# The first tile's early store, the late weights and the zeroes of a two-expert combine

## The chip, the cores and the metric

The kernel runs on one core of one Trainium2 chip. The metric is device time in microseconds (us) of the slowest core, which here is the only one. The kernel before took 238.82 us, the median of 3 runs (238.82 to 239.0).

## The reference

Each of 16 x 1024 = 16384 tokens has the output rows of two experts (k = 2), 512 float32 values each, and two weights. The result is the weighted sum of the two rows.

```python
# expert_outputs (16, 1024, 2, 512), combine_weights (16, 1024, 2), float32
weights = combine_weights[..., np.newaxis]
return np.sum(expert_outputs * weights, axis=2).astype(np.float32)
```

The inputs are 67.1 MB and the output is 33.6 MB, so 100.8 MB cross between HBM and SBUF, with two multiplications and one addition for each output value.

## The kernel before, in words

**Layout.** The 128 partitions hold 128 tokens each. A partition's tokens t = 0 to 114 ("main") are neighbours in HBM; the last 13 tokens of each partition come from a second block behind the first. A tile is 13 (or 12) tokens of every partition: 10 tiles, g = 0 to 9, of 13, 13, 12, 13, 13, 13, 12, 13, 13 and 13 tokens. One big SBUF tensor, `et`, has four rooms of 13, 13, 12 and 13 tokens; tile g lives in room g mod 4. So tiles 0 to 3 are loaded at the start, and tile g + 4 can only be loaded when the store of tile g has read its results out of the room. The results stand in the room itself: the sums are written, packed, to its first half. `halves` is the same tensor seen as rows of 512 values, two to a token.

**Engines and queues.** SP issues all the loads (line 76), in five pieces at first (2, 11, 13, 12, 13 tokens: the first tile is cut in two), then one for each tile from 4 to 9, each behind the store that frees its room. SP's DMAs are queue q1 of the profile. ACT (ScalarE) issues, on queue q10, a small store of zeroes to 16 places of the output that are overwritten later (line 111), the weights of tiles 0 to 8 (line 79, called on line 112), the weights of tile 9 in two halves of 64 partitions (line 114), a warm-up activation (line 115), and the stores of tiles 0 to 6 (line 130). The stores of tiles 7 and 8 together, and of tile 9, go out on SP instead. The zeroes are set by DVE (VectorE) on line 108.

**Arithmetic.** Tiles 0 to 7 ("WHOLE") take two DVE instructions each: a product of all the tile's values with the weights, in place (line 88), and a sum of the two halves of each token (line 97). Tile 8 ("MIXED") has part of its products on ACT (line 92) and the rest on DVE (lines 94 and 96). Tile 9 goes token by token: ACT scales one half (line 102), DVE multiplies the other and adds (line 103).

**Order.** The program order is written out by hand (`manual_schedule`): the zeroes, the weights, the five first loads, and then for each store in the list `STORES` its tile's arithmetic, the store, and the load into the room that it frees. Each engine runs its own part of that list in order; semaphores hold an instruction until what it needs has landed or has been read.

Of the kernel before, what the change touches and what calls it, by code (L numbers as in the profile page):

```python
# [1 line left out]

# [4 lines left out]


@with_exitstack
def kernel(  # L10
    ctx: ExitStack,
    tc: tile.TileContext,
    expert_outputs: bass.AP,
    combine_weights: bass.AP,
    out: bass.AP,
):

    nc = tc.nc
    b, s, k, h = expert_outputs.shape
    assert k == 2
    n = b * s
    P = nc.NUM_PARTITIONS
    per = n // P
    assert per * P == n

    ROOM = [13, 13, 12, 13]
    ROOMS = len(ROOM)  # L30
    SITE = [sum(ROOM[:i]) for i in range(ROOMS)]
    TILES = [13, 13, 12, 13, 13, 13, 12, 13, 13, 13]
    FIRST = [2, 11, 13, 12, 13]
    STORES = [[0], [1], [2], [3], [4], [5], [6], [7, 8], [9]]
    WHOLE = [0, 1, 2, 3, 4, 5, 6, 7]
    MIXED = [8]
    ALONE = 3
    FREE = {9: 0}
    LAST = 13
    assert all(c <= ROOM[g % ROOMS] for g, c in enumerate(TILES))  # L40
    assert sum(TILES) == per and [g for st in STORES for g in st] == list(range(len(TILES)))
    main = per - LAST
    starts = [sum(TILES[:g]) for g in range(len(TILES))]

    def rows(x):

        first = x[0 : P * main, :].rearrange("(p t) f -> p t f", p=P)
        second = x[P * main : n, :].rearrange("(p t) f -> p t f", p=P)
        return lambda t, c: first[:, t : t + c, :] if t < main else second[:, t - main : t - main + c, :]

    flat = out.rearrange("b s h -> (b s) h")
    eo = rows(expert_outputs.rearrange("b s k h -> (b s) (k h)"))
    cw = rows(combine_weights.rearrange("b s k -> (b s) k"))
    o = rows(flat)

    dt = mybir.dt.float32
    mult = mybir.AluOpType.mult
    add = mybir.AluOpType.add
    copy = mybir.ActivationFunctionType.Copy

    pool = ctx.enter_context(tc.tile_pool(name="all", bufs=1))
    et = pool.tile([P, sum(ROOM), k * h], dt)
    halves = et.rearrange("p j (k h) -> p (j k) h", k=k)
    wt = pool.tile([P, per * k], dt)
    wk = wt.rearrange("p (t k) -> p t k", k=k)
    zt = pool.tile([16, 128], dt)
    warm = pool.tile([P, 1], dt)

    def place(t):
        g = max(g for g in range(len(TILES)) if starts[g] <= t)  # L70
        return SITE[g % ROOMS] + t - starts[g]

    def load(t, c, **kw):
        at = place(t)
        assert place(t + c - 1) == at + c - 1
        nc.sync.dma_start(out=et[:, at : at + c], in_=eo(t, c), **kw)  # L76

    def weights(q, t, c):
        q.dma_start(out=wk[:, t : t + c, :], in_=cw(t, c))

    def combine(g, base):
        at, c, t0 = SITE[g % ROOMS], TILES[g], starts[g]
        if g in WHOLE or g in MIXED:
            room = halves[:, k * at : k * (at + c), :]
            x0, x1 = et[:, at : at + c, 0:h], et[:, at : at + c, h : 2 * h]
            if g in WHOLE:
                wb = wt[:, k * t0 : k * (t0 + c)].unsqueeze(2).to_broadcast([P, k * c, h])
                nc.vector.tensor_tensor(out=room, in0=room, in1=wb, op=mult)  # L88
            else:
                for i in range(ALONE, c):  # L90
                    x = et[:, at + i, 0:h]
                    nc.scalar.activation(out=x, in_=x, func=copy, scale=wt[:, k * (t0 + i) : k * (t0 + i) + 1])  # L92
                w1 = wk[:, t0 : t0 + c, 1:2].to_broadcast([P, c, h])
                nc.vector.tensor_tensor(out=x1, in0=x1, in1=w1, op=mult)  # L94
                w0 = wk[:, t0 : t0 + ALONE, 0:1].to_broadcast([P, ALONE, h])
                nc.vector.tensor_tensor(out=x0[:, 0:ALONE], in0=x0[:, 0:ALONE], in1=w0, op=mult)  # L96
            nc.vector.tensor_tensor(out=halves[:, base : base + c, :], in0=x0, in1=x1, op=add)  # L97
            return
        for i in range(c):
            t = k * (t0 + i)  # L100
            x0, x1 = halves[:, k * (at + i), :], halves[:, k * (at + i) + 1, :]
            nc.scalar.activation(out=x0, in_=x0, func=copy, scale=wt[:, t : t + 1])  # L102
            nc.vector.scalar_tensor_tensor(  # L103
                out=halves[:, base + i, :], in0=x1, scalar=wt[:, t + 1 : t + 2], in1=x0, op0=mult, op1=add
            )

    with tc.manual_schedule():
        nc.vector.memset(zt, 0.0)  # L108

        ahead = flat[0 : P * main, :].rearrange("(q t) h -> q (t h)", q=16)  # L110
        nc.scalar.dma_start(out=ahead[:, 0:128], in_=zt)  # L111
        weights(nc.scalar, 0, main)
        for half in (slice(0, P // 2), slice(P // 2, P)):
            nc.scalar.dma_start(out=wk[half, main:per, :], in_=cw(main, per - main)[half])
        nc.scalar.activation(out=warm, in_=nc.const_aps.tensor(1.0, (P, 1), dt), func=copy)  # L115

        t = 0
        for i, c in enumerate(FIRST):
            load(t, c, **({"max_dma_last_dim": k * h * 4} if i == 0 else {}))
            t += c  # L120
        assert t == sum(TILES[:ROOMS])
        for j, st in enumerate(STORES):
            room = FREE.get(st[0], st[0] % ROOMS)
            base, c = SITE[room] * k, 0
            for g in st:
                combine(g, base + c)
                c += TILES[g]
            assert c <= k * ROOM[room]
            q = nc.sync if j in (7, 8) else nc.scalar
            q.dma_start(out=o(starts[st[0]], c), in_=halves[:, base : base + c, :])  # L130
            for g in st:
                if g + ROOMS < len(TILES):
                    load(starts[g + ROOMS], TILES[g + ROOMS])


# [1 line left out]
_INS = ['expert_outputs', 'combine_weights']  # L137
_OUTS = [((16, 1024, 512), 'float32')]


# [23 lines left out]
```

## Time and profile before

| what | value |
|---|---|
| time, median of 3 runs | 238.82 us (238.82 to 239.0) |
| profiled execution: span from first to last instruction | 237.1 us |
| HBM read, written | 67.24 MB, 33.56 MB |
| DVE busy in the span | 190.0 us |
| ACT busy in the span | 15.8 us |

Of the profiled execution the span is all that is recorded; its own time as a run is not listed. The 1.7 us between its span and the median of the runs lie before the first instruction and after the last one.

How to read it: times are microseconds from the start of the span unless marked ns. A row of the timeline or the groups names the engine, the line of the kernel, the operation, what is written from what, and the shapes. ACTq and SPq are the instructions by which ACT and SP issue DMAs. "To landing" is the time from a DMA's issue until its last byte and its semaphore have arrived. The windows view gives, for a stretch of the span, the busy time of each engine, the mean busy share of the 16 DMA engines, and the GB/s that they moved. It counts a packet where it starts, so that short stretches come out lumpy: a packet here can be one partition's whole row of a tile.

### The profile page before, as it was taken

How to read it: one execution, taken by the hardware profiler on the slowest of the kernel's cores; microseconds unless marked ns; L12 is line 12 of the kernel's file. 1: busy time of each engine (PE TensorE's matmuls, PEld its weight loads, DVE VectorE, ACT ScalarE, POOL GpSimd, SP SyncE). 2: the span in 40 equal slices, each digit the busy share in tenths (PEclk: the TensorE clock that was granted, in tenths of full speed). 3: DMA queues.
4: the chain of work that ended last, by engine and by line, in shares of the span. 5: the costliest groups of instructions: out<-in, count | busy, mean ns of one | idle time of the engine just before them, and what ended most of it. 6: DMA issues, size and time to landing. Idle time of an engine off the chain costs nothing.

```text
span 237.1 us, 154 instructions
## 1 busy us (share of the span) xinstructions
DVE 190.0 (80%) x33; ACT 15.8 (7%) x25; POOL 0.2 (0%) x4
## 2 busy tenths in 40 slices
DVE  0006999999999999999999998998499969919400
ACT  2000000000000000000000000000000055019200
POOL 0000000000000000000000000000000000000000
DMA  8999999989999999999899999999899999899996
GB/s 300 388 481 434 432 421 398 470 348 485 449 431 458 431 440 390 486 420 420 359 492 409 409 509 392 431 503 431 359 431 503 420 397 483 381 431 431 431 431 287
DMA packets 3344, 100.80 MB, mean 425 GB/s; under 512 B 512, under 2 KB 656, under 8 KB 912
## 3 DMA queue, kind: packets, MB, share of 16 engines
q1 hardware_dynamic: 2000, 77.33, 75.9%
q10 hardware_dynamic: 1344, 23.47, 23.0%
HBM read 67.24 MB, written 33.56 MB: 425 GB/s over the span
## 4 chain that ended last, share of the span: by engine, by line
DVE 55%; DMA 36%; issue 1%; ACT 0%; DVEq 0%; ACTq 0%; SPq 0%
DVE et L88 35%; DVE et L97 17%; DMA out_dram<-et 17%; DMA et<-in_expert_outputs_dram 12%; DMA wt<-in_combine_weights_dram 8%; DVE et L103 3%; ACT et L102 0%; DVEq L159 0%; ACTq L111 0%; DVE zt L108 0%; DVEq L88 0%; SPq L76 0%; ACTq L102 0%
## 5 line engine op out<-in xcount | busy, mean ns | idle before, releaser
L88 DVE TENSOR_TENSOR et<-et,wt 128x13312 f32<-128x13312 f32 (+1 forms) x8 | 110.0, 13754 | 23.8 <-DMA wt<-in_combine_weights_dram 18.7
L97 DVE TENSOR_TENSOR et<-et 128x6656 f32<-128x6656 f32 (+1 forms) x9 | 62.8, 6973 | 0.4
L92 ACT ACTIVATE et<-et,wt 128x512 f32<-128x512 f32 x10 | 6.2, 708 | 188.0 <-DMA et<-in_expert_outputs_dram 188.0
L103 DVE SCALAR_TENSOR_TENSOR et<-et,wt 128x512 f32<-128x512 f32 x13 | 8.7, 747 | 5.0 <-ACT et L102 5.0
L102 ACT ACTIVATE et<-et,wt 128x512 f32<-128x512 f32 x13 | 8.1, 707 | 14.0 <-DMA et<-in_expert_outputs_dram 14.0
L94 DVE TENSOR_TENSOR et<-et,wt 128x6656 f32<-128x6656 f32 x1 | 7.1, 7093 | 2.3 <-DMA et<-in_expert_outputs_dram 2.3
L96 DVE TENSOR_TENSOR et<-et,wt 128x1536 f32<-128x1536 f32 x1 | 1.8, 1751 | 0.0
L115 ACT ACT_TABLE_LOAD x1 | 1.3, 1283 | 3.1 <-issue 3.1
L108 DVE MEMSET zt<- 16x128 f32 x1 | 0.2, 165 | 0.8 <-PEq L148 0.8
L115 ACT ACTIVATE warm<-const-float32-1.0 128x1 f32<-128x1 f32 x1 | 0.2, 203 | 0.0
L148 POOL MEMSET const-bfloat16-1.0<- 128x1 bf16 x1 | 0.1, 102 | 0.0
L148 POOL MEMSET const-uint8-127<- 128x1 uint8 x1 | 0.1, 101 | 0.0
L148 POOL MEMSET const-float32-0.0<- 128x1 f32 x1 | 0.1, 99 | 0.2 <-issue 0.2
L148 POOL MEMSET const-float32-1.0<- 128x1 f32 x1 | 0.1, 98 | 0.0
## 6 DMA issues: line engine op xcount, KB each, us to landing
et<-in_expert_outputs_dram SPq DMA_DIRECT2D x7, 6656.0 KB, 32.2
out_dram<-et ACTq DMA_DIRECT2D x5, 3328.0 KB, 34.7
et<-in_expert_outputs_dram SPq DMA_DIRECT2D x2, 6144.0 KB, 41.1
out_dram<-et SPq DMA_DIRECT2D x1, 6656.0 KB, 19.9
out_dram<-et ACTq DMA_DIRECT2D x2, 3072.0 KB, 37.2
et<-in_expert_outputs_dram SPq DMA_DIRECT2D x1, 5632.0 KB, 18.2
out_dram<-et SPq DMA_DIRECT2D x1, 3328.0 KB, 14.0
et<-in_expert_outputs_dram SPq DMA_DIRECT2D x1, 1024.0 KB, 5.0
```

The costliest lines, as they stand in the source:

```text
L88: nc.vector.tensor_tensor(out=room, in0=room, in1=wb, op=mult)
L92: nc.scalar.activation(out=x, in_=x, func=copy, scale=wt[:, k * (t0 + i) : k * (t0 + i) + 1])
L94: nc.vector.tensor_tensor(out=x1, in0=x1, in1=w1, op=mult)
L96: nc.vector.tensor_tensor(out=x0[:, 0:ALONE], in0=x0[:, 0:ALONE], in1=w0, op=mult)
L97: nc.vector.tensor_tensor(out=halves[:, base : base + c, :], in0=x0, in1=x1, op=add)
L102: nc.scalar.activation(out=x0, in_=x0, func=copy, scale=wt[:, t : t + 1])
L103: nc.vector.scalar_tensor_tensor(out=halves[:, base + i, :], in0=x1, scalar=wt[:, t + 1 : t + 2], in1=x0, op0=mult, op1=add)
L108: nc.vector.memset(zt, 0.0)
L115: nc.scalar.activation(out=warm, in_=nc.const_aps.tensor(1.0, (P, 1), dt), func=copy)
L148: nc = _bacc.Bacc("TRN2", target_bir_lowering=False, num_devices=1)
```

## The change

Three edits, all in the first tile and the set-up.

1. The first tile's first 3 tokens (`EARLY`) get a product and a sum of their own and are stored by ACT at once. The product, the sum and the store for the other 10 tokens follow. The store's two parts go to the same places of the output as the one store did.
2. The weights of the last tile are loaded by one DMA of 128 partitions, issued by ACT right behind the second part of the first tile's store, in place of two DMAs of 64 partitions at the start.
3. The zeroes are set by GpSimd (POOL in the profile) in place of DVE.

The rest of the diff moves the same instructions into helpers (`products`, `sums`, `store`); for tiles 1 to 9 they are the same instructions in the same order.

```diff
+    EARLY = 3
...
+    def products(room, t, c):
+        wb = wt[:, k * t : k * (t + c)].unsqueeze(2).to_broadcast([P, k * c, h])
+        nc.vector.tensor_tensor(out=room, in0=room, in1=wb, op=mult)
+
+    def sums(at, c, base):
+        x0, x1 = et[:, at : at + c, 0:h], et[:, at : at + c, h : 2 * h]
+        nc.vector.tensor_tensor(out=halves[:, base : base + c, :], in0=x0, in1=x1, op=add)
+
-    def combine(g, base):
-        at, c, t0 = SITE[g % ROOMS], TILES[g], starts[g]
+    def combine(g, base, done=0):
+        at, c, t0 = SITE[g % ROOMS] + done, TILES[g] - done, starts[g] + done
+        if g in WHOLE:
+            products(halves[:, k * at : k * (at + c), :], t0, c)
+            sums(at, c, base)
+            return
...
+    def store(q, t, base, c):
+        q.dma_start(out=o(t, c), in_=halves[:, base : base + c, :])
+
     with tc.manual_schedule():
-        nc.vector.memset(zt, 0.0)
-
+        nc.gpsimd.memset(zt, 0.0)
         ahead = flat[0 : P * main, :].rearrange("(q t) h -> q (t h)", q=16)
         nc.scalar.dma_start(out=ahead[:, 0:128], in_=zt)
         weights(nc.scalar, 0, main)
-        for half in (slice(0, P // 2), slice(P // 2, P)):
-            nc.scalar.dma_start(out=wk[half, main:per, :], in_=cw(main, per - main)[half])
         nc.scalar.activation(out=warm, in_=nc.const_aps.tensor(1.0, (P, 1), dt), func=copy)
...
+        early = EARLY
+        products(halves[:, k * SITE[0] : k * (SITE[0] + early), :], 0, early)
+        sums(SITE[0], early, k * SITE[0])
+        store(nc.scalar, 0, k * SITE[0], early)
         for j, st in enumerate(STORES):
             room = FREE.get(st[0], st[0] % ROOMS)
             base, c = SITE[room] * k, 0
+            done = early if j == 0 else 0
             for g in st:
-                combine(g, base + c)
+                combine(g, base + c + done, done)
                 c += TILES[g]
...
-            q = nc.sync if j in (7, 8) else nc.scalar
-            q.dma_start(out=o(starts[st[0]], c), in_=halves[:, base : base + c, :])
+            store(nc.sync if j in (7, 8) else nc.scalar, starts[st[0]] + done, base + done, c - done)
+            if j == 0:
+                weights(nc.scalar, main, per - main)
```

More of the change, by code (lines that the diff above doesn't have):

```diff
@@ L79, in weights @@
         q.dma_start(out=wk[:, t : t + c, :], in_=cw(t, c))
-    def combine(g, base):
-        at, c, t0 = SITE[g % ROOMS], TILES[g], starts[g]
-        if g in WHOLE or g in MIXED:
-            room = halves[:, k * at : k * (at + c), :]
-            x0, x1 = et[:, at : at + c, 0:h], et[:, at : at + c, h : 2 * h]
[L86 to L97, printed above, removed]
+    def products(room, t, c):
+        wb = wt[:, k * t : k * (t + c)].unsqueeze(2).to_broadcast([P, k * c, h])
+        nc.vector.tensor_tensor(out=room, in0=room, in1=wb, op=mult)
```

9 lines of the change are left out of this document (added).

## The prediction, on record before the result

> **What bounds the kernel now.** I read the page first: its span, its slices and its queues.
>
> ```profile
> span 237.1 us, 154 instructions
> DVE 190.0 (80%) x33; ACT 15.8 (7%) x25; POOL 0.2 (0%) x4
> DMA  8999999989999999999899999999899999899996
> DMA packets 3344, 100.80 MB, mean 425 GB/s; under 512 B 512, under 2 KB 656, under 8 KB 912
> q1 hardware_dynamic: 2000, 77.33, 75.9%
> q10 hardware_dynamic: 1344, 23.47, 23.0%
> ```
>
> DVE is busy for 80% of the span, but the DMA engines for 75.9 + 23.0 = 98.9%. The windows view cuts off the ends and tells where the missing 1.1% lies (columns: window, length, DVE, ACT and POOL busy, clock, DMA share, GB/s).
>
> ```profile
> 2.00:235.70 233.70, 189.85 (x32) 15.79 (x25) 0.00 (x0) 1.00 1.00 431
> 235.70:237.10 1.40, 0.00 (x0) 0.00 (x0) 0.00 (x0) 1.00 0.00 0
> 213.00:222.00 9.00, 8.44 (x13) 7.88 (x13) 0.00 (x0) 1.00 1.01 438
> 43.40:45.70 2.30, 2.30 (x1) 0.00 (x0) 0.00 (x0) 1.00 0.96 342
> ```
>
> From 2.0 to 235.7 us the DMA share is 1.00 at 431 GB/s. So the span is 2.0 us of start, 233.7 us of transfers without a hole, and 1.4 us of end. The chain of waits names DVE for much of the span; I don't follow it, because a saved microsecond of DVE leaves the same bytes to be moved. The time can fall only if the bytes move faster or the ends shrink, and can rise only if the engines stand idle or get more work.
>
> The second thing to see is how the two queues share the engines. These are rows of the DMA view (KB each, us to landing), and q1 and q10 in the window 20.5 to 36 us (packets, MB, share).
>
> ```profile
> et<-in_expert_outputs_dram SPq DMA_DIRECT2D x1, 5632.0 KB, 18.2
> wt<-in_combine_weights_dram ACTq DMA_DIRECT2D x1, 115.0 KB, 18.2
> wt<-in_combine_weights_dram ACTq DMA_DIRECT2D x2, 6.5 KB, 31.0
> out_dram<-zt ACTq DMA_DIRECT2D x1, 8.0 KB, 3.9
> et<-in_expert_outputs_dram SPq DMA_DIRECT2D x7, 6656.0 KB, 32.2
> out_dram<-et SPq DMA_DIRECT2D x1, 6656.0 KB, 19.9
> ...
> q1 hardware_dynamic: 144, 6.75, 100.6%
> q10 hardware_dynamic: 144, 0.01, 0.7%
> ```
>
> 115 KB of weights land as late as 5632 KB of data, and in 15.5 us both queues start 144 packets, though one moves 6.75 MB and the other 0.01. The engines take turns, a packet from each queue, whatever its size: a tiny row waits for one big row of the other queue. 144 packets are 9 for each of 16 engines, for 128 rows 8 and one completion. At 431 GB/s, 26.9 for an engine, a row of a 13-token load (53,248 B) takes 1.98 us, of its store half of that, 0.99 us, of a 12-token load 1.83 us and store 0.91 us.
>
> **The change, part by part.** The rows for DVE and for the issues (start, us, what; idle time in brackets):
>
> ```profile
> 0.33 0.10 POOL L148 MEMSET const-uint8-127<- 128x1 uint8 x1
> 0.81 0.17 DVE L108 MEMSET zt<- 16x128 f32 x1 [0.81 <-PEq L148]
> 1.91 1.16 ACTq L114 DMA_DIRECT2D wt<-in_combine_weights_dram  x2
> 19.73 14.02 DVE L88 TENSOR_TENSOR et<-et,wt 128x13312 f32<-128x13312 f32 x1 [18.75 <-DMA wt<-in_combine_weights_dram]
> 33.78 7.09 DVE L97 TENSOR_TENSOR et<-et 128x6656 f32<-128x6656 f32 x1
> 40.91 0.34 ACTq L130 DMA_DIRECT2D out_dram<-et  x1
> 61.86 12.95 DVE L88 TENSOR_TENSOR et<-et,wt 128x12288 f32<-128x12288 f32 x1
> 74.84 6.56 DVE L97 TENSOR_TENSOR et<-et 128x6144 f32<-128x6144 f32 x1
> 145.69 12.96 DVE L88 TENSOR_TENSOR et<-et,wt 128x12288 f32<-128x12288 f32 x1 [1.10 <-DMA et<-in_expert_outputs_dram]
> 169.18 14.03 DVE L88 TENSOR_TENSOR et<-et,wt 128x13312 f32<-128x13312 f32 x1 [3.94 <-DMA et<-in_expert_outputs_dram]
> 192.63 7.09 DVE L94 TENSOR_TENSOR et<-et,wt 128x6656 f32<-128x6656 f32 x1 [2.30 <-DMA et<-in_expert_outputs_dram]
> 199.64 1.75 DVE L96 TENSOR_TENSOR et<-et,wt 128x1536 f32<-128x1536 f32 x1
> ```
>
> *DVE.* 14.02 against 12.95 us is 1.04 ns a value and 0.1 to 0.2 us fixed. Products of 3 and 10 tokens then take 3.4 and 10.8 us; sums 1.75 (the 1536-value row) and 5.5 us (7.09 against 6.56 gives the same slope). Together 21.4 against 21.1 us: +0.3 us for every later tile. The wait of 1.10 us before tile 6, then 3.94 and 2.30 us, hide it; without them it would cost 0.3 us.
>
> *The early store.* Its arithmetic starts at 19.73 as before (token 2 comes with the 11-token load), so ACT issues it at 24.9, and the other 10 tokens' at 41.2. Neither adds bytes. It adds 128 rows, 8 for an engine. What a row costs beyond its bytes the trace doesn't list. From below it is nothing. From above: at the best stretch's 438 GB/s, 100.8 MB take 230.1 us of the 233.7; put the whole rest, 3.6 us, on 3344 / 16 = 209 packets, and it is 0.017 us each, 0.14 us for 8. I take 0.1. The number of DMAs stays the same (one store more, one weight load less). A small gain can't be excluded: at 43.4 to 45.7, where the first store's rows begin, the rate is 342, worth (431 - 342) / 431 x 2.3 = 0.5 us. The early store may only move that hitch; I count it at 0 and keep 0.5.
>
> *The last weights.* Two issues of together 1.16 us leave ACT's start, where only the warm-up stands behind them. Their 128 rows need as many turns as before, 9, but now in q10 behind the first tile's store and ahead of tile 1's. That has to be followed:
>
> ```profile
> q10 hardware_dynamic: 15, 0.40, 92.5%
> ...
> 61.97 0.34 ACTq L130 DMA_DIRECT2D out_dram<-et  x1
> 67.80 0.33 SPq L76 DMA_DIRECT2D et<-in_expert_outputs_dram  x1
> 81.43 0.34 ACTq L130 DMA_DIRECT2D out_dram<-et  x1
> 91.42 0.33 SPq L76 DMA_DIRECT2D et<-in_expert_outputs_dram  x1
> 123.44 14.02 DVE L88 TENSOR_TENSOR et<-et,wt 128x13312 f32<-128x13312 f32 x1
> 208.61 14.02 SPq L130 DMA_DIRECT2D out_dram<-et  x2
> 183.92 28.80 DMA et<-in_expert_outputs_dram
> 212.72 0.02 issue
> ```
>
> The first row is q10 between 45 and 46 us: the store issued at 40.91 starts its rows there, 4.8 us after its issue. So the early store starts near 30 and, with 8 turns of 1.9 + 0.23 us, is through by about 47. The second part follows, 8 turns of 1.9 + 0.76 us: about 68, where the whole store landed before (SP's refill of room 0 goes out at 67.80). Then the weights hold q10 for their 8 rows with 7 load rows of 1.98 us between, 14 us, to 82. Tile 1's store, issued near 62.3, had its turns from 68 on; now it starts 14 us later. In those 14 us the loads have the engines nearly alone. Four of tile 4's rows are in by 82 and the other four, in turns with tile 1's store (2.97 us each), by 94, instead of 67.8 + 32.2 = 100. Then SP has nothing to load until tile 1's store is in: its last 4 rows run unshared, to 98 (before: 91.4). The load of tile 5 goes out at 98 and starts between 99 (1 us later, an estimate) and 103 (4.8 us, as above); tile 2's store, issued at 81.8, holds 8 x 0.91 = 7.3 us of rows, to 105. So the engines have work throughout. With 8 turns of 1.98 + 0.95 us tile 5 is in between 122.5 and 126.5, against 123.8 on DVE (123.44 + 0.3): at worst 2.7 us late, which the same three waits (7.3 us) hide. From there the old rhythm runs on.
>
> *The zeroes.* POOL's rows show 0.10 us for a memset of 128x1, DVE's 0.17 us for this one; on POOL it may take 0.1 to 1.3 us (the longest small instruction here, ACT's table load, is under 1.3 us). If the weights lose a turn by it, DVE starts 1.7 us later (an 11-token row); the waits of 1.10 + 3.94 + 2.30 = 7.3 us hide that. Loads don't wait for the zeroes. Counted at 0.
>
> *The end.* The last load lands at 212.72. The stores of tiles 7 and 8 have been issued at 208.61, 4.1 us ahead, and tile 9's goes out 14.0 us later, at 222.3, while the pair's 6656 KB land 19.9 us after their issue, at 228.5. So DVE could be late by 7.3 + 4.1 = 11.4 us at tile 1 before the engines ran dry here.
>
> Sum: 0 (DVE) + 0.1 (rows) + 0 (weights) + 0 (zeroes) = +0.1 us on the span of 237.1, and with the same 1.7 us outside it, 238.9 us.
>
> **The rivals.**
>
> *Faster: the hitch of the first store goes.* For it: the 342 GB/s row. Against: a first store remains, and packets of 2 us make so short a window lumpy. Worth 0.5 us, or up to 0.7 if the end also gets shorter: 238.3, 238.1 at best.
>
> *Slower: the parked weights starve the rooms.* Place: ACT's queue from 68 to 82 us. If tile 1's store and with it tile 5's load lose the whole hold, and the unshared stretches give nothing back, the hold is 13.5 us (the 6.5 KB rows landed 31.0 us after about 2.2, at 33.2; the weights ahead of them at 19.6). DVE then starts tile 5 13.5 us late; 11.4 are covered, 2.1 are not: 240.9. It decides once tile 5's load lands after 123.8 + 11.4 = 135.2 us; each microsecond beyond costs one. Against it: turns of a queue without a partner are free, by the share of 1.00.
>
> *Slower: a new wait.* If the product of the 10 tokens were held until the early store has read room 0, DVE would stand from 24.9 to 47, 22 us, of which 11.4 are covered: 249.5. Against it: the store reads half-rows 0 to 2, the product writes 6 to 25 and the sum 3 to 12; and in the old trace DVE goes on in `et` beside a running store.
>
> *Slower: the extra store costs engine time.* As a whole small DMA it could cost what the 8 KB store took, 3.9 us: 242.7. Against it: the program's 24 DMAs would hold the engines for 94 us, and only 3.6 us in all are unaccounted. By the Trainium skill ("DMA: Bandwidth & Descriptors", Anatomy of one DMA) a DMA has about 2.0 us fixed beside its bytes, measured on GpSimd's path, and its Bandwidth section advises transfers of 1 MiB and more; the early store has 0.75 MiB, and the sum by that would be 240.8. The trace disagrees for queued transfers: it has no room for such a cost.
>
> *The change doesn't do what it says:* if the early rows only queue behind loads, nothing is written earlier that matters; the time is that of the forecast.
>
> **How the numbers follow.** Forecast (nothing idles) 0.52, 238.4 to 239.3; hitch gone 0.20; parked weights 0.20, from 239.3 to 240.9; new wait 0.04; engine time 0.04. 0.2%, 0.48 us, is about what a measurement of this kernel can tell from no change. So faster 0.20, same 0.52, slower 0.28. The range 238.1 to 240.2 takes in the hitch and the lower half of the parked weights; outside are that case's upper half (0.10) and the two dear ones (0.08).
>
> **What would show it.** Right: a DMA share of 1.00 between 2.0 and 235.7 us again; the early store issued near 24.9; tile 1's store with a far longer time to landing (36 instead of 29 us); tile 5's load landing before 127; the waits before tiles 6 to 8 within 2 us of the old ones. Wrong: windows under 0.97 around 94 to 106 us (starved), a DVE gap at 25 (new wait), or a short stretch of over 431 GB/s near 30 and 45 with an earlier end (hitch gone).

## The result and the profile after

| | before | changed |
|---|---|---|
| time, median of 10 runs each | 238.88 us (238.82 to 239.0) | 239.52 us (239.41 to 239.65) |
| span of the profiled execution | 237.1 us | 237.8 us |
| ratio, with its 95% interval | 1 | 1.0027 (1.0018 to 1.0036) |

The changed kernel is slower by 0.64 us. The forecast was 238.9 and the range 238.1 to 240.2; the time lies in the range, and 0.27% is just past the 0.2% that counted as no change. Ratios here are formed on undisturbed runs alone, so they can differ a little from the ratio of two medians.

The page after, for the lines that were read before:

```profile
span 237.8 us, 157 instructions
DVE 190.2 (80%) x34; ACT 15.8 (7%) x25; POOL 0.4 (0%) x5
DMA packets 3472, 100.80 MB, mean 424 GB/s; under 512 B 512, under 2 KB 656, under 8 KB 1040
q1 hardware_dynamic: 2000, 77.33, 75.8%
q10 hardware_dynamic: 1472, 23.47, 23.0%
```

The bytes are the same and the packets 128 more, as many as the cut store adds rows. The windows:

```profile
2.00:235.70 233.70, 190.16 (x34) 15.64 (x25) 0.00 (x0) 1.00 1.00 431
2.00:236.30 234.30, 190.16 (x34) 15.64 (x25) 0.00 (x0) 1.00 1.00 430
94.50:101.00 6.50, 6.47 (x2) 0.00 (x0) 0.00 (x0) 1.00 1.01 434
```

The DMA engines have no hole: their share stays at 1.00 until 0.6 us later, with the same bytes. So the loss is for the most part in how long rows take, and not in engines that stand idle; how large a part is worked out further down. The third row is the stretch in which SP has nothing to load: the stores alone keep the share at 1.01.

The timeline after, with the issues (start, us, what, idle time before):

```profile
19.72 3.36 DVE L84 TENSOR_TENSOR et<-et,wt 128x3072 f32<-128x3072 f32 x1 [19.72 <-DMA wt<-in_combine_weights_dram]
24.91 16.60 ACTq L116 DMA_DIRECT2D out_dram<-et  x2
41.53 0.46 ACTq L80 DMA_DIRECT2D wt<-in_combine_weights_dram  x1
...
97.70 0.33 SPq L77 DMA_DIRECT2D et<-in_expert_outputs_dram  x1
...
125.85 14.03 DVE L84 TENSOR_TENSOR et<-et,wt 128x13312 f32<-128x13312 f32 x1 [2.06 <-DMA et<-in_expert_outputs_dram]
148.22 12.96 DVE L84 TENSOR_TENSOR et<-et,wt 128x12288 f32<-128x12288 f32 x1 [1.22 <-DMA et<-in_expert_outputs_dram]
171.72 14.03 DVE L84 TENSOR_TENSOR et<-et,wt 128x13312 f32<-128x13312 f32 x1 [3.95 <-DMA et<-in_expert_outputs_dram]
195.00 7.09 DVE L102 TENSOR_TENSOR et<-et,wt 128x6656 f32<-128x6656 f32 x1 [2.13 <-DMA et<-in_expert_outputs_dram]
210.99 12.25 SPq L116 DMA_DIRECT2D out_dram<-et  x2
```

DVE starts at 19.72 as before, the early store is issued at 24.91, tile 5's load at 97.70. DVE now waits 2.06 us for that load, and the three old waits are as long as they were. The next rows are the DMA view after: landings, q1 and q10 in the window 68 to 81 us, and q10 alone in 94.5 to 101.

```profile
out_dram<-et ACTq DMA_DIRECT2D x1, 768.0 KB, 21.6
wt<-in_combine_weights_dram ACTq DMA_DIRECT2D x1, 13.0 KB, 42.3
...
q1 hardware_dynamic: 112, 5.11, 90.8%
q10 hardware_dynamic: 112, 0.01, 0.7%
...
q10 hardware_dynamic: 128, 2.82, 100.7%
```

In 13 us the late weights take 112 turns against 112 packets of q1 (5.11 MB, so 96 load rows of 53,248 B, and 16 completion marks): they hold q10 while 0.01 MB move.

Most of what the engines lost is in the first store's place. Below stand q1's rows in two windows, 43 to 45.5 and 45.6 to 48 us, before and then after. Each window holds one load row for each of the 16 engines (16 packets, 0.79 MB), so the share times the window's length is the mean duration of a row: 1.82 us undisturbed, for a 12-token load.

```profile
q1 hardware_dynamic: 16, 0.79, 88.1%
q1 hardware_dynamic: 16, 0.79, 77.1%
```

```profile
q1 hardware_dynamic: 16, 0.79, 87.9%
q1 hardware_dynamic: 16, 0.79, 91.9%
```

Before: 0.881 x 2.5 = 2.20 us and 0.771 x 2.4 = 1.85. After: 2.20 and 0.919 x 2.4 = 2.21. The hitch that one round of load rows had is now in two rounds, 0.36 us more.

### The profile page after: what moved, and what is told of

Same layout as the page of the kernel before. It is cut to its first block, busy times and chain, and to the rows that moved or that the text cites. A ratio compares the mean times of both kernels' runs of the same rounds, so it can differ in the third digit from the quotient of the medians.

```text
span 237.8 us, 157 instructions
## 1 busy us (share of the span) xinstructions
DVE 190.2 (80%) x34; ACT 15.8 (7%) x25; POOL 0.4 (0%) x5
## 4 chain that ended last, share of the span: by engine, by line
DMA 62%; DVE 30%; ACT 0%; DVEq 0%; issue 0%; ACTq 0%; POOLq 0%; SPq 0%
DMA out_dram<-et 30%; DMA et<-in_expert_outputs_dram 25%; DVE et L84 18%; DVE et L88 9%; DMA wt<-in_combine_weights_dram 8%; DVE et L111 3%; ACT et L110 0%; DVEq L173 0%; ACTq L121 0%; POOLq L173 0%; DVEq L84 0%; SPq L77 0%; ACTq L110 0%; POOLq L162 0%
## 5 line engine op out<-in xcount | busy, mean ns | idle before, releaser
L84 DVE TENSOR_TENSOR et<-et,wt 128x13312 f32<-128x13312 f32 (+3 forms) x9 | 110.2, 12244 | 27.0 <-DMA wt<-in_combine_weights_dram 19.7
L88 DVE TENSOR_TENSOR et<-et 128x6656 f32<-128x6656 f32 (+3 forms) x10 | 62.9, 6292 | 0.4
```

## The experiments

The question was what doubles the hitch. **Theory A:** the weights' DMA, issued by ACT 0.4 us behind the store. **Theory B:** the early store. Row durations in the tables are worked out as above, from the same two windows.

### First group: one part at a time

The early store alone (before, with the product, sum and store of 3 tokens added):

```diff
+        products(halves[:, k * SITE[0] : k * (SITE[0] + early), :], 0, early)
+        sums(SITE[0], early, k * SITE[0])
+        store(nc.scalar, 0, k * SITE[0], early)
```

> The kernel before with the early store alone; the last weights stay in two halves at the start, DVE sets the zeroes. Theory A (each DMA that ACT issues near 41 us lengthens one round of load rows, so the second long round comes from the weights' issue behind the store): one long round, near 43.5 us, rows of 2.2 us there and 1.8 to 1.9 at 46; time within 0.2 us of before. Theory B (the early store itself causes the second long round): long rounds at 43.5 and 46 us, time 0.4 to 0.6 us above before.

The late weights alone:

```diff
-        for half in (slice(0, P // 2), slice(P // 2, P)):
-            nc.scalar.dma_start(out=wk[half, main:per, :], in_=cw(main, per - main)[half])
...
+            if j == 0:
+                weights(nc.scalar, main, per - main)
```

> The kernel before with the last weights in one DMA behind the first tile's whole store; no early store, DVE sets the zeroes. Theory A: two long rounds of load rows (43.5 and 46 us), time 0.4 to 0.6 us above before. Theory B: one long round, time within 0.2 us of before. Rival C (the parked weights cost, by lateness of the rooms and not by long rows): one long round, and time up to 0.6 us above before through idle DMA engines.

Ten tokens early:

```diff
-    EARLY = 3
+    EARLY = 10
```

> The changed kernel with 10 tokens early and 3 behind them: ACT issues the big part near 36 us and the small part and the weights near 41. Theory A (issues near 41 with a small store still count): long rounds near 43.5 and 46 us as with 3. Theory D (a long round belongs to the first store with big rows, about 2.5 us behind its issue): the first long round moves to about 38.5 us. A fixed time in the span: long rounds stay at 43.5 us. Time 239.0 to 239.6 us on a chip where before takes 238.9.

The changed kernel with its weights at the start:

```diff
         weights(nc.scalar, 0, main)
+        weights(nc.scalar, main, per - main)
...
-            if j == 0:
-                weights(nc.scalar, main, per - main)
```

> The changed kernel (early store, zeroes on GpSimd) with the last weights in one DMA at the start, behind the other weights. Theory A: one long round near 43.5 us, time within 0.2 us of before. Theory B: two long rounds, 0.4 to 0.6 us above before, like the changed kernel.

| kernel | time, us (before: 238.83) | ratio | interval | row at 43 to 45.5 | row at 45.6 to 48 |
|---|---|---|---|---|---|
| early store alone | 240.20 | 1.0058 | 1.0045 to 1.0071 | 1.82 | 1.81 |
| late weights alone | 239.64 (239.24 to 240.0) | 1.0033 | 1.0021 to 1.0046 | 2.46 | 1.83 |
| 10 tokens early | 239.31 | 1.0024 | 1.0015 to 1.0033 | 1.82 | 1.82 |
| changed, weights at the start | 240.70 | 1.0075 | 1.0062 to 1.0087 | 1.82 | 1.82 |

Neither theory came out, and C neither: with late weights alone the profiled DMA share is 1.00 from 2.0 to 235.7 us. The parts don't add: the early store alone costs 1.4 us, the late weights alone 0.8, both together (with GpSimd's zeroes) 0.64. With weights at the start the early store waits behind them in q10, the first tile's second part lands later, and the refill of room 0 goes out at 73.5 us (early store alone) and 73.7 us (changed, weights at the start) instead of 67.8.

In these two runs the store is cut as in the changed kernel, and neither window has a long round. The early store alone, q1 at 43 to 45.5 and 45.6 to 48 us, and then at 52 to 54.5 and 68 to 82 us:

```profile
q1 hardware_dynamic: 16, 0.79, 72.6%
q1 hardware_dynamic: 16, 0.79, 75.6%
...
q1 hardware_dynamic: 16, 0.85, 87.7%
q1 hardware_dynamic: 63, 2.50, 45.8%
```

The third line is the round directly before the second part's first rows (issued at 40.88, first row at 54.79 us): 0.877 x 2.5 = 2.19 us for a 13-token row, against 1.97 undisturbed. In the last window 47 load rows (2.50 MB) took 0.458 x 14 x 16 = 102.6 us of engine time in place of 47 x 1.966 = 92.4, which is 0.64 us on a mean engine. So a cut store doesn't always give two long rounds near 44 and 46 us; here the long rows lie elsewhere, and there are more of them.

In the same two runs the end also runs dry for a moment. The kernel with weights at the start, windows and timeline:

```profile
212.20:213.00 0.80, 0.00 (x0) 0.00 (x0) 0.00 (x0) 1.00 0.16 67
```

```profile
212.17 0.35 SPq L116 DMA_DIRECT2D out_dram<-et  x1
```

The store of tiles 7 and 8 is issued at 212.17, 3.6 us later than before (early store alone: 211.80). The share of 0.16 says that hardly a row starts in these 0.8 us, while rows begun earlier still run. Added up from the start and duration of each packet, a mean engine stands idle between 212 and 214 us for 0.54 us here and for 0.20 us with the early store alone, of 1.8 and 1.4 us that the spans are longer. The rest is the longer rows and a few late engines: the sixteen completion marks of the last store, one for each DMA engine, lie between 237.03 and 238.10 us with the middle one at 237.12 (early store alone: 236.68, 237.73, 236.76; before: 235.98, 236.33, 236.11). So with the last weights ahead of it the early store costs more than twice as much as with the weights behind the first store or left out (the second group).

With 10 tokens early the long rounds move: one row directly before the first store row near 38 us, and one at 50.9 to 53.4 us of 2.50 us (16 rows, share 99.9% of 2.5 us). So they belong to the store (D, for the first of them) and to no fixed time. D puts the long round 2.5 us behind the issue; in the early store alone it came some 11 us behind, so it goes with the first rows and not with the issue.

### Second group: the weights moved or left out

To clear theory A, the changed kernel without any late weights (its last tile uses the first tile's):

```diff
-            if j == 0:
-                weights(nc.scalar, main, per - main)
...
-            t = k * (t0 + i)
+            t = k * i
```

> The changed kernel without any load of the last tile's weights: the last tile is computed with the first tile's weights instead, so its values are not the reference's. Theory A (the weights' issue behind the store lengthens the load rows near 46 us, and their place in the queue makes the rooms late): long rows near 43.5 us only, store of tiles 7 and 8 issued near 208.7 us as before, time within 0.2 us of before. Theory E (long rows come from the first store with big rows meeting loads while the 16 DMA engines are in step; the weights are innocent): long rows near 43.5 and 46 us as in the changed kernel, 0.3 to 0.6 us above before.

The weights one store later:

```diff
-            if j == 0:
+            if j == 1:
                 weights(nc.scalar, main, per - main)
```

> The changed kernel with the last weights behind the store of tile 1 instead of tile 0's. Theory A: long rows near 43.5 us only, the room of tile 5 not late (its load issued near 91 us), time within 0.3 us of before. Theory E: long rows near 43.5 and 46 us, 0.3 to 0.6 us above before.

The kernel before without them (the two halves' DMAs are left out, and `t = k * i` as above):

> The kernel before without any load of the last tile's weights: the last tile is computed with the first tile's weights instead, so its values are not the reference's. If the 0.8 us of the run with late weights and no early store came from the weights' issue or place (A): 238.8 us, long rows of 0.4 us on average near 43.5 as before. If the tiny rows of the two halves between 20 and 36 us were of use (they put the engines out of step) and their going is the cause (E): 0.2 to 0.8 us above before, with long rows of 0.6 us on average.

The weights on SP's queue:

```diff
         assert t == sum(TILES[:ROOMS])
+        weights(nc.sync, main, per - main)
```

> The changed kernel with the last weights on SP's queue right behind the five first loads, so that ACT's queue has only the stores. Theory A: like f1, within 0.2 us of before. Theory E: 0.3 to 0.6 us above before, with the long rows of the changed kernel. Rooms in both: load of tile 5 issued near 91 us, store of tiles 7 and 8 near 208.7.

| kernel | time, us (before: 238.89) | ratio | interval | row at 43 to 45.5 | row at 45.6 to 48 |
|---|---|---|---|---|---|
| changed, no late weights | 239.45 | 1.0022 | 1.0005 to 1.0040 | 2.25 | 2.12 |
| changed, weights behind tile 1's store | 239.55 | 1.0021 | 1.0001 to 1.0042 | 2.31 | 2.22 |
| before, no late weights | 238.98 | 1.0000 | 0.9984 to 1.0017 | 2.34 | 1.83 |
| changed, weights on SP | 243.94 | 1.0188 | 1.0153 to 1.0222 | 2.25 | 2.16 |

Theory A falls, and E's forecast of the rows holds: without any late weights both rounds stay long. That engines in step are the condition, as E has it, no run shows. First the changed kernel, then the kernel before, both without late weights, q1 in the two windows:

```profile
q1 hardware_dynamic: 16, 0.79, 89.8%
q1 hardware_dynamic: 16, 0.79, 88.4%
```

```profile
q1 hardware_dynamic: 16, 0.79, 93.7%
q1 hardware_dynamic: 16, 0.79, 76.1%
```

The tiny rows of the two halves, from 20 to 36 us, were of little use either: without them the first round is 0.14 us longer (2.34 against 2.20) and the time 0.1 us longer, which the interval doesn't tell from nothing.

The weights on SP were the surprise: 5 us above before, 4.5 above the changed kernel without them. There they stand ahead of tile 4's load in q1 and take their turns against tile 1's store. Tile 4 lands late, DVE waits 3.25 us for it, and everything behind it is late to the end. Its windows and timeline:

```profile
213.60:217.60 4.00, 3.30 (x1) 0.08 (x1) 0.00 (x0) 1.00 0.03 13
```

```profile
216.92 0.35 SPq L116 DMA_DIRECT2D out_dram<-et  x1
```

The store of tiles 7 and 8 goes out at 216.92, when most engines have long been through with the last load, and for 4 us they stand at a share of 0.03. That is the point from which lateness costs.

### Third group: the time of the early store, or its cut

Now two theories were left for the doubled hitch. **F:** cutting the store in two does it, whenever the parts are issued. **G:** the early rows do it, by breaking into the loads ahead of time. The first two kernels here leave the late weights out, as above, and keep the two-part arithmetic.

The call of the early store moved behind the arithmetic of the other 10 tokens, so that both parts should go out near 41 us:

```diff
-        store(nc.scalar, 0, k * SITE[0], early)
...
+            if j == 0:
+                store(nc.scalar, 0, k * SITE[0], early)
             store(nc.sync if j in (7, 8) else nc.scalar, starts[st[0]] + done, base + done, c - done)
```

> As the changed kernel without the last weights (the last tile uses the first tile's weights, so its values are not the reference's), but both parts of the first tile's store are issued back to back near 41 us, when all 13 tokens are done. Theory F (the hitch doubles when q10 gets two DMAs at the first store, whatever their time): long rows of together 0.7 to 0.9 us for an engine between 42 and 50 us, 0.4 to 0.7 us above before. Theory G (it doubles because the early rows have already broken into the loads): long rows of 0.4 to 0.55 us together, within 0.25 us of before.

One store:

```diff
-        store(nc.scalar, 0, k * SITE[0], early)
...
-            store(nc.sync if j in (7, 8) else nc.scalar, starts[st[0]] + done, base + done, c - done)
+            store(nc.sync if j in (7, 8) else nc.scalar, starts[st[0]], base, c)
```

> As the changed kernel without the last weights (the last tile uses the first tile's weights, so its values are not the reference's), with the first tile's arithmetic in two parts as changed but one store for all 13 tokens. Theories F and G both: one long round of 0.4 to 0.55 us for an engine near 43.5 us, within 0.25 us of before (238.8 to 239.1). If it is 0.4 us or more above before, the cost sits in DVE's two more instructions or in GpSimd's zeroes, and not in the store.

The two other edits alone, merged and on GpSimd, with the weights at the start:

```diff
-        nc.vector.memset(zt, 0.0)
+        nc.gpsimd.memset(zt, 0.0)
...
-        for half in (slice(0, P // 2), slice(P // 2, P)):
-            nc.scalar.dma_start(out=wk[half, main:per, :], in_=cw(main, per - main)[half])
+        weights(nc.scalar, main, per - main)
```

> The kernel before with the last weights in one DMA at the start in place of two, and the zeroes on GpSimd; the first tile is stored whole. Prediction's sum: both are free, within 0.2 us of before. If merging or GpSimd cost: more than 0.3 us above before.

The late weights alone, behind tile 3's store (`if j == 3`, from the late weights of the first group):

> The kernel before with the last weights in one DMA behind the store of tile 3 (issued near 102.5 us). Theory F (a second DMA beside the first store doubles the hitch, so the weights cost 0.8 us only there): one long round of 0.4 to 0.55 us near 43.5, within 0.3 us of before. Theory H (parked weights cost by making the later rooms late, wherever they stand): 0.4 to 1.0 us above before, with the store of tiles 7 and 8 issued 2 us later than 208.6.

| kernel | time, us (before: 238.85) | ratio | interval | row at 43 to 45.5 | row at 45.6 to 48 |
|---|---|---|---|---|---|
| two parts, call of the first moved | 239.54 | 1.0026 | 1.0016 to 1.0035 | 2.31 | 2.15 |
| two-part arithmetic, one store | 238.94 | 0.9995 | 0.9979 to 1.0011 | 2.44 | 1.84 |
| merged weights at the start, zeroes on GpSimd | 238.93 | 1.0002 | 0.9993 to 1.0011 | 2.40 | 1.83 |
| weights behind tile 3's store | 238.96 | 1.0004 | 0.9995 to 1.0013 | 2.37 | 1.85 |

The first of these runs doesn't do what its expectation says. The edit moves the call in the program's text, but between the two places ACT has nothing else to run, and it issued the early store as soon as the three tokens were done, at 24.87 us (24.91 in the changed kernel). ACT's timeline at 24 to 26 and 40 to 43 us:

```profile
24.87 0.34 ACTq L116 DMA_DIRECT2D out_dram<-et  x1
41.14 0.34 ACTq L116 DMA_DIRECT2D out_dram<-et  x1
```

So it repeats the changed kernel without late weights (239.54 here, 239.45 there, rows 2.31 and 2.15 against 2.25 and 2.12) and doesn't tell F from G. No run here does. What the group shows is the early store in two parts against one store, with the same arithmetic and without late weights: 239.54 - 238.94 = 0.60 us. Two stores, then one store, q1 in the two windows and at 26 to 34 us:

```profile
q1 hardware_dynamic: 16, 0.79, 92.3%
q1 hardware_dynamic: 16, 0.79, 89.7%
q1 hardware_dynamic: 64, 3.41, 101.2%
```

```profile
q1 hardware_dynamic: 16, 0.79, 97.4%
q1 hardware_dynamic: 16, 0.79, 76.7%
q1 hardware_dynamic: 64, 3.41, 98.4%
```

Against one store the second round is 0.31 us longer but the first 0.13 shorter, so the two windows hold only 0.18 of the 0.60 us. At 26 to 34 us, where the early store's rows begin, the load rows take 1.012 x 8 x 16 / 64 = 2.02 us against 1.97, with 4 rows for an engine 0.22 us. The 128 rows more are 0.06 us (worked out below). That makes 0.46, and the middle mark of the last store is 0.49 us later (236.47 against 235.98); the last mark is 0.72 later (236.95 against 236.23), so some 0.23 us of this profiled execution are engines behind the others.

The early arithmetic, the merged weights and GpSimd's zeroes are free, and so are the parked weights behind tile 3's store (Theory H falls). No version tried beats the kernel before; the best are level with it.

Three things stay open. Whether the cut of the store or its early rows lengthen the load rows: a kernel in which ACT really holds the early store back until 41 us wasn't run. Why load rows lengthen near a store's first rows at all, the trace doesn't tell: it shows no resource below a row's duration. And the late weights alone, right behind an uncut first store, took 0.8 us at the median with one long round of 2.46 us and none after (1.83); its profiled execution had a span of 237.5 us, 0.4 above before, so what its slower runs lost is in no trace.

## Why the prediction was right or wrong

- **The bound.** Right. Share 1.00 up to the end, and a loss that DVE's 0.2 us more of work has no part in: the one-store kernel has the same arithmetic and 238.94 us.
- **The rows of the early store, 0.1 us.** Right in size: 128 packets more are 8 for an engine. The trace's packets give 0.008 us each beyond their bytes (26,624 B in 0.987 us, 53,248 B in 1.966), 0.06 us.
- **The hitch.** This is the step that failed: "The early store may only move that hitch; I count it at 0 and keep 0.5". The sign was open and only a gain was kept as an end. In the changed kernel it neither moved nor went, it got a second round: +0.36 us on a mean engine. What the experiments show in place of the 0 is 0.60 us for the early store in two parts against one store, spread over several load rows; whether the cut or the early time does it stays open.
- **The rest.** 0.06 + 0.36 = 0.42 of 0.61 us in the span. In the trace the sixteen completion marks of the last store fall between 235.98 and 236.33 us before and between 236.33 and 236.92 after. The middle one is 0.45 us later, the last one 0.59. So some 0.14 us are one engine behind the others, which makes 0.56.
- **The late weights.** The walk through q10 was right nearly row by row. Early store issued at 24.9 (24.91), refill of room 0 "about 68" (68.09), tile 1's store in at 98 (its refill goes out at 97.70), tile 5's load between 122.5 and 126.5 (it lands at 125.75, just ahead of DVE's 125.85), engines without a hole between. As a rival, parked weights were given 0.20 and 240.9; in the changed kernel they cost some 0.1 us by the medians (239.52 against 239.45 without them, in another set of runs), which the intervals don't separate from nothing.
- **The cover of 11.4 us.** Wrong, and hidden by the small delay. The prediction took the waits of 1.10, 3.94 and 2.30 us as slack that a late DVE uses up. After, DVE is 2.4 us late at tile 5 (125.85 against 123.44), waits 1.22, 3.95 and 2.13 us all the same, and issues the store of tiles 7 and 8 2.4 us late (210.99 against 208.61). A late tile makes its store late, that store's room, and that room's load: the waits move with the delay. The real cover is the lead of that store over the last load:

```profile
182.32 31.01 DMA et<-in_expert_outputs_dram
213.33 0.02 issue
```

  (the chain of waits after). Counted to the slowest engine's landing, it was 4.1 us and is 2.3. With the weights at the start it is 2.3 too (212.17 to 214.50), and yet the engines run dry there:

```profile
183.32 31.18 DMA et<-in_expert_outputs_dram
214.50 0.02 issue
```

  That landing is the slowest engine's. The sixteen marks lie between 212.47 and 214.50 us, the middle one at 212.59, and the store's first rows start at 213.0, 0.8 us behind the issue. So the cover has to be counted to the middle engine and less these 0.8 us; before, that is 212.50 - 0.8 - 208.61 = 3.1 us, an estimate, in place of 11.4. Lateness of 2.4 us (changed) stayed under it, 3.2 and 3.6 us (the two runs with the weights at the start) went past it by a little, and 8.3 us (weights on SP) by some 4 us of idle engines.
- **A new wait, engine time.** Right to give them little: DVE goes from 23.11 to 41.05 without a gap. By the Trainium skill ("DMA: Bandwidth & Descriptors", Bandwidth and Anatomy of one DMA) small DMAs are to be avoided and have some 2.0 us fixed, measured on GpSimd's path. The direction agrees with this case, the size doesn't: the store more costs 0.60 us here, and the measurement decides.
- **The chances.** Slower had 0.28, but for causes that weren't the one. The time missed the forecast's own band (238.4 to 239.3) and lies in the range only because that was widened for parked weights, which by the medians cost some 0.1 us here. That was luck. A second rival on the hitch, with the opposite sign, was missing.

## What to carry to other kernels

Where the DMA engines are full from start to end, sending a part of a result earlier moves no bytes faster; here it only added turns and disturbances. So look for what a change makes the engines do and not for what it makes the compute engines wait. An idle time before a load isn't slack when that load hangs, through a room and a store, on the same engine's earlier work; follow the ring once round before you count it as cover. And a small anomaly in a window, such as a slow stretch where a store begins, has two signs: put both into the range. Last, moving a call in the program's text moves nothing in time when its engine has no other work between the two places; before an experiment is read, the trace must show that its edit took effect.

## What the runs showed of the hardware

- A row of 104 B waits for a turn like one of 53 KB: 112 packets each in 13 us, and 13 KB of weights took 42.3 us to land. The place in which such rows stand decides the cost: 0.1 us behind tile 3's store, which the interval doesn't tell from nothing, 0.8 us at the median behind an uncut first store, and 4.5 us on the loads' own queue (243.94 against 239.45 without them).
- The DMA engines don't stay in step. Tile 6's load lands on the sixteen engines between 145.24 and 145.59 us before and between 146.57 and 148.13 after, and with the weights on SP the last load lands between 213.40 and 217.44. A load counts when the last engine is through, so one engine a turn behind delays the whole room. The Trainium skill ("DMA: Bandwidth & Descriptors", Why a DMA increments its semaphore by 16 and not by 1) says that the engines finish independently and that only the full count means landed; the trace agrees, with these spreads.
- In all six kernels here that store the first tile whole, one round of load rows directly before the store's first rows takes 0.4 to 0.65 us longer (rows of 2.20 to 2.46 us against 1.82). With the store in two parts, long rows come in two rounds near 44 and 46 us in five kernels and in other places in three.
- The first rows of tiles 7 and 8's store start 0.8 us behind its issue when the engines have nothing else to do (212.17 to 213.0 with the weights at the start, 216.92 to 217.8 with the weights on SP).
